# Attention over 128-token heads: output stores paired from step 8 on, and the last product cut 24 to 8

## The chip, the cores and the metric

The kernel runs on one core of a Trainium2 chip. The metric is the time of one execution on the device, in microseconds (us). The kernel before has a median of 131.08 us over five executions (130.66 to 132.13).

The core has five engines that work side by side and are held together by semaphores: TensorE (PE in the profile, with its weight loads as PEld), VectorE (DVE), ScalarE (ACT), GpSimd (POOL) and SyncE (SP), which here does nothing but issue transfers. Transfers between HBM and the on-chip memory run on 16 DMA engines. A transfer is issued by SP, ACT or POOL; in the profile the packets of SP's transfers stand under queue 1, ACT's under queue 10 and POOL's under queue 0.

## What is computed

```python
batch, n_heads, seq, head_dim = 32, 12, 128, 64      # q, k, v: float32
scale = 1.0 / np.sqrt(q.shape[-1])
scores = scale * np.matmul(q, k.transpose(0, 1, 3, 2))
scores_max = np.max(scores, axis=-1, keepdims=True)
attn = np.exp(scores - scores_max)
attn = attn / (np.sum(attn, axis=-1, keepdims=True) + 1e-8)
return np.matmul(attn, v).astype(np.float32)
```

There are 384 independent heads of 128 tokens by 64 features. Each of q, k, v and the output is 12.58 MB in float32. The kernel takes the exponential without subtracting the maximum.

## The kernel before

The 384 heads are worked off in 12 steps of 32 heads (`NDUO` = 12, so the last step is `e` = 11). In each step a tile has 128 partitions, and each partition holds 32 tokens of 64 features (`TQ` = 32). A step's output tile `o_sb` is therefore 128 x 2048 float32, 1 MB, and one store moves it (8 KB in each partition).

**Loads.** POOL issues the loads of q and k (L57) and of v (L65), which turn float32 into bf16 on the way: 512 KB arrive on the chip for every 1 MB that is read. Only the first q and k come as float32, over SP and ACT (L72). The later loads are issued by the list `later` (L99), one entry at the end of each of steps 0 to 6; the last, q11 and k11, is issued at the end of step 6.

**A step m** (the loop at L207) runs, in the order in which it is written: the first half of the scores of step m+1 (TensorE, L119, with the exponential on ACT, L124); the sums of the exponentials (TensorE L150, DVE transposes and takes the reciprocal, L172 and L174); the two halves of the output (TensorE L160, DVE transposes each into `o_sb`, L179), with the second half of the scores of step m+1 between them; pieces of the rearrangement of v for a later step (TensorE L139, ACT copies them out at L143); the transposes of q and k of step m+2 on DVE (L107); the loads of `later`; and last, POOL multiplies the whole `o_sb` by the reciprocals (L183), and some finished tiles are stored (L188).

The whole is written with a manual schedule: each engine carries out its own instructions in the order in which the program states them. An instruction that issues a store stands in the queue of the engine that issues it, and waits there for the product of the tile that it stores.

**Stores.** `held` (L192, L193) says which finished steps are stored at the end of step m, all issued by ACT:

```python
held = {m: [m - LAG] for m in range(LAG, e - 2)}      # LAG = 5, e = 11
held[e - 2], held[e - 1] = [e - 7, e - 6], [e - 5, e - 4]
```

So steps 5, 6, 7 and 8 issue the stores of tiles 0, 1, 2 and 3, step 9 those of tiles 4 and 5, and step 10 those of tiles 6 and 7. Tiles 8, 9 and 10 are stored in the last step by SP (L234, L235), which has nothing else queued: each of these is issued as soon as POOL has multiplied its tile, however early in time that is.

**The last step** cuts the product of tile 11 in two halves of 16 tokens: the first on DVE, the second on POOL (L232, L233). Each half is stored by itself, 512 KB: the first by ACT, the second by SP (L236, L237).

The tiles `o_sb` lie in a pool of `LAG + 3` = 8 buffers, shared with the two float32 loads at the start; tile m+8 reuses the buffer of tile m.

Of the kernel before, what the change touches and what calls it, by code (L numbers as in the profile page):

```python
# [10 lines left out]
def kernel(  # L11
# [12 lines left out]
    nc = tc.nc  # L24
# [6 lines left out]
    TQ = 32  # L31
# [5 lines left out]
    LAG = 5  # L37
# [31 lines left out]
    with tc.manual_schedule():  # L69
# [5 lines left out]
        def load(names):  # L75
            for name in names.split():
                kind, m = name[0], int(name[1:])
                load_v(m) if kind == "v" else load_qk(m, "qk".index(kind))
# [23 lines left out]
        def turn(m, which):  # L102


            x = chunks.pop((m, which)).bitcast(f32)
            xt = pt.tile([128, 8, S], f32, tag="qk"[which] + "t", name="qk"[which] + "t")
            nc.vector.transpose(  # L107
                xt.rearrange("p h (x g) -> p x h g", g=4),
                x if which == 0 else x.rearrange("p (y t) e -> p t y e", t=T))
            qts[m, which] = xt.bitcast(bf16).rearrange("p h (s j) -> p h s j", j=2)  # L110

        def scores(m, i):
            qt, kt = qts[m, 0], qts[m, 1]
            s_ps = ps.tile([128, 4, 4, S], f32, tag="s_ps", name="s_ps")
            for h in range(4):
                for j in range(2):
                    for b in range(4):
                        pr = slice(b * 32, (b + 1) * 32)
                        nc.tensor.matmul(  # L119
                            s_ps[:, b, h, :], lhsT=kt[pr, 4 * i + h, :, j],  # L120
                            rhs=qt[pr, 4 * i + h, :, j],
                            start=(j == 0), stop=(j == 1), tile_position=(b * 32, 0))
            attn = pa.tile([128, 4, 4, S], bf16, tag="attn", name="attn")
            nc.scalar.activation(out=attn, in_=s_ps, func=mybir.ActivationFunctionType.Exp,  # L124
                                 bias=0.0, scale=scale)
            attns[m, i] = attn

        def values(m, a, heads, half):


            v_bf = chunks[m, 2]
            ns = slice(0, 2 * CB) if half is None else slice(half * CB, (half + 1) * CB)
            if m not in v2s:
                v2s[m] = pa.tile([128, A, 2 * CB, D], bf16, tag="v2", bufs=2, name="v2")
            v_ps = ps.tile([128, heads, 4 * CB // heads, D], f32, tag="w_ps", bufs=2, name="v_ps")
            for i in range(heads):
                for tl in range(2):
                    for u in range(4):
                        nc.tensor.matmul(  # L139
                            v_ps[u * 32:(u + 1) * 32, i], lhsT=perm[:, a + i, tl, :],  # L140
                            rhs=v_bf[:, ns, 2 * u + tl, :], start=(tl == 0), stop=(tl == 1),
                            tile_position=(0, u * 32))
            nc.scalar.copy(v2s[m][:, a:a + heads, ns], v_ps)  # L143

        def denominators(m):

            d_ps = ps.tile([128, 8, S], f32, tag="w_ps", bufs=2, name="d_ps")
            for i in range(2):
                for b in range(4):
                    nc.tensor.matmul(  # L150
                        d_ps[b * 32:(b + 1) * 32, 4 * i:4 * i + 4], lhsT=ones,
                        rhs=attns[m, i][:, b], start=True, stop=True, tile_position=(0, b * 32))
            return d_ps

        def outputs(m, j):

            o_ps = ps.tile([128, 8, S], f32, tag="w_ps", bufs=2, name="o_ps")
            for h in range(8):
                for b in range(4):
                    nc.tensor.matmul(  # L160
                        o_ps[b * 32:(b + 1) * 32, h],
                        lhsT=v2s[m // 2][:, h, 4 * (m % 2) + b, j * 32:(j + 1) * 32],
                        rhs=attns[m, h // 4][:, b, h % 4],
                        start=True, stop=True, tile_position=(0, b * 32))
            return o_ps
# [4 lines left out]
        def divide(m, d_ps):  # L170
            dt = pf.tile([128, TQ, 32], f32, tag="dt", name="dt")
            nc.vector.transpose(dt, turned(d_ps))  # L172
            recip = pf.tile([128, TQ], f32, tag="recip", bufs=6, name="recip")
            nc.vector.reciprocal(recip, dt[:, :, 0])  # L174
            osbs[m] = (po.tile([128, TQ, D], f32, tag="o_sb", name="o_sb"), recip)

        def finish(m, j, o_ps):
            o_sb, _ = osbs[m]
            nc.vector.transpose(o_sb[:, :, j * 32:(j + 1) * 32], turned(o_ps))  # L179

        def scale_rows(m, eng, lo, hi):
            o_sb, recip = osbs[m]
            eng.tensor_mul(o_sb[:, lo:hi], o_sb[:, lo:hi],  # L183
                           recip[:, lo:hi].to_broadcast([128, hi - lo, D]))

        def store(m, eng, lo=0, hi=TQ):
            o_sb, _ = osbs[m]
            eng.dma_start(out=orr[:, m, lo * D:hi * D],  # L188
                          in_=o_sb[:, lo:hi].rearrange("p t d -> p (t d)"))

        e = NDUO - 1
        held = {m: [m - LAG] for m in range(LAG, e - 2)}  # L192
        held[e - 2], held[e - 1] = [e - 7, e - 6], [e - 5, e - 4]  # L193
        shuffles = {0: [(0, 0, 4, 1), (0, 4, 4, 1)],
                    1: [(1, a, 2, None) for a in range(0, A, 2)]}
        for m in range(2, NDUO // 2):
# [10 lines left out]
        for m in range(NDUO):  # L207
            todo = shuffles.get(m, [])
            if m < e:
                scores(m + 1, 0)  # L210
            divide(m, denominators(m))
            if len(todo) > 3:
                values(*todo.pop(0))
            finish(m, 0, outputs(m, 0))
            if len(todo) > 1:
                values(*todo.pop(0))
            if m < e:
                scores(m + 1, 1)
            finish(m, 1, outputs(m, 1))
            for x in todo:  # L220
                values(*x)
            if m + 2 <= e:
                turn(m + 2, 0)
                turn(m + 2, 1)
            if m < len(later):
                load(later[m])
            if m < e:
                scale_rows(m, nc.gpsimd, 0, TQ)
                for s in held.get(m, []):
                    store(s, nc.scalar)  # L230
            else:
                scale_rows(m, nc.vector, 0, TQ // 2)  # L232
                scale_rows(m, nc.gpsimd, TQ // 2, TQ)  # L233
                for s in range(e - 3, e):  # L234
                    store(s, nc.sync)  # L235
                store(m, nc.scalar, 0, TQ // 2)  # L236
                store(m, nc.sync, TQ // 2, TQ)  # L237


# [28 lines left out]
```

## Time and profile before

| What | Value |
|---|---|
| median of 5 executions | 131.08 us |
| the five | 130.66, 131.87, 132.13, 131.03, 131.08 |
| the profiled execution | 130.66 us, of which the span from first to last instruction is 128.8 us |
| busy time in the span | PE 68.5, PEld 41.5, DVE 77.7, ACT 70.7, POOL 64.4 us |
| read from HBM, written to it | 37.75 MB, 12.58 MB |
| mean granted TensorE clock | 0.885 |

Times in the trace count from the start of the span. The busy time of an engine is the time in which it carries out instructions; issuing a transfer and waiting do not count. "DMA share" is the mean busy share of the 16 DMA engines in a stretch; it can stand a little over 1 where packets overlap. "GB/s" counts the bytes at the destination, so the loads, which halve their data on the way, show about 210 GB/s where the stores show about 410.

These are the issues of all output stores, from the trace (tile, issuing engine, time of issue in us, us from issue to landing):

| Tile | By | Issued | To landing |
|---|---|---|---|
| 0 | ACT | 72.55 | 10.0 |
| 1 | ACT | 78.91 | 8.4 |
| 2 | ACT | 90.09 | 10.8 |
| 3 | ACT | 96.44 | 10.1 |
| 8 | SP | 100.53 | 7.7 |
| 4 | ACT | 107.08 | 4.0 |
| 5 | ACT | 107.46 | 8.0 |
| 9 | SP | 109.71 | 8.8 |
| 6 | ACT | 111.75 | 8.6 |
| 7 | ACT | 112.18 | 11.8 |
| 10 | SP | 117.20 | 8.1 |
| 11, first half | ACT | 121.15 | 5.4 |
| 11, second half | SP | 122.91 | 4.9 |

The last load, k11, is issued at 75.84 and lands 30.8 us later, at 106.67.

### The profile page before, as it was taken

To read this page: it belongs to the slowest core of one execution; us is meant where nothing else is said; L and a number is where in the kernel's file an instruction comes from. 1 tells how busy PE (TensorE), PEld (TensorE's weight loads), DVE (VectorE), ACT (ScalarE), POOL (GpSimd) and SP (SyncE) were. 2 spreads that over 40 slices of the span, in tenths; PEclk is the share of its full clock that TensorE was granted. 3 is DMA by queue.
4 is the path that set the end of the run, shared out by engine and by line. 5 is a ranking of instruction groups with operands and counts; after the bars stand their busy time and mean duration, and the time that the engine had idled before them with its cause. 6 is when DMAs were issued, how large, how long until landed. Compare 5 with 4: busy or idle time off the path is not lost.

```text
span 128.8 us, 4462 instructions
## 1 busy us (share of the span) xinstructions
PE 68.5 (53%) x2080; PEld 41.5 (32%) x2080; DVE 77.7 (60%) x79; ACT 70.7 (55%) x51; POOL 64.4 (50%) x52
## 2 busy tenths in 40 slices
PE   0001976657675638865189564686562886624000
PEld 0001654523333424534055251442342443413000
DVE  0128338646275968558946869557597575929600
ACT  3023795927667734977455868538673587720000
POOL 6921131316935997196692864603709209073710
PEclk9999999977999995999958999779998599995555
DMA  4999999999999999999999999999999986999990
GB/s 86 414 253 217 204 218 212 204 211 214 201 212 215 214 209 210 212 211 215 208 204 219 214 261 318 294 282 215 218 307 276 360 323 265 417 425 399 415 399 33
DMA packets 11683, 32.80 MB, mean 255 GB/s; under 512 B 784, under 2 KB 6928, under 8 KB 10000
## 3 DMA queue, kind: packets, MB, share of 16 engines
q0 software_dynamic: 9504, 17.83, 74.3%
q10 hardware_dynamic: 1440, 9.96, 19.2%
q1 hardware_dynamic: 720, 4.72, 9.5%
q8 instruction: 16, 0.26, 0.7%
q14 instruction: 3, 0.02, 0.0%
HBM read 37.75 MB, written 12.58 MB: 391 GB/s over the span
## 4 chain that ended last, share of the span: by engine, by line
DVE 35%; PE 23%; DMA 18%; ACT 7%; issue 6%; POOL 4%; POOLq 2%; ACTq 0%; DVEq 0%
DMA v_bf<-in_v_dram 18%; DVE o_sb L179 12%; PE s_ps L119 9%; DVE kt L107 8%; DVE qt L107 8%; DVE dt L172 7%; PE v_ps L139 7%; ACT attn L124 6%; PE d_ps L150 4%; PE o_ps L160 4%; POOLq L263 2%; POOL v_bf L65 1%; POOL q_bf L57 1%; POOL k_bf L57 1%; ACT v L143 1%
## 5 line engine op out<-in xcount | busy, mean ns | idle before, releaser
L124 ACT ACTIVATE attn<-s_ps 128x2048 bf16<-128x2048 f32 x24 | 45.1, 1879 | 22.8 <-PE s_ps L119 22.8
L183 POOL TENSOR_TENSOR o_sb<-o_sb,recip 128x2048 f32<-128x2048 f32 (+1 forms) x12 | 42.7, 3562 | 27.9 <-DVE o_sb L179 24.0
L119 PE MATMUL s_ps<-qt,kt 32*128 32x128 bf16 x768 | 17.1, 229 | 37.8 <-DVE kt L107 31.4
L179 DVE STREAM_TRANSPOSE o_sb<-o_ps 128x1024 f32<-128x1024 f32 x24 | 28.9, 1215 | 11.2 <-PE o_ps L160 11.2
L139 PE MATMUL v_ps<-v_bf,perm 128*32 128x512 bf16 (+1 forms) x448 | 28.9, 387 | 6.4 <-DVE dt L172 2.9
L143 ACT CAST v<-v_ps 128x1024 bf16<-128x1024 f32 x24 | 24.0, 1017 | 12.4 <-PE v_ps L139 12.4
L119 PEld LDWEIGHTS <-kt 32*128 32x128 bf16 x768 | 13.0, 98 | 46.4 <-DVE kt L107 36.1
L172 DVE STREAM_TRANSPOSE dt<-d_ps 128x1024 f32<-128x1024 f32 x12 | 15.0, 1249 | 20.7 <-PE d_ps L150 20.7
L160 PE MATMUL o_ps<-attn,v 128*32 128x128 bf16 x768 | 18.1, 239 | 3.0 <-issue 2.2
L139 PEld LDWEIGHTS <-perm 128*32 128x32 bf16 x448 | 13.4, 105 | 17.1 <-issue 12.7
L160 PEld LDWEIGHTS <-v 128*32 128x32 bf16 x768 | 14.4, 106 | 8.3 <-issue 5.5
L107 DVE STREAM_TRANSPOSE qt<-q_bf 128x1024 f32<-128x1024 f32 x12 | 14.5, 1208 | 1.2 <-DMA q_bf<-in_q_dram 1.2
L107 DVE STREAM_TRANSPOSE kt<-k_bf 128x1024 f32<-128x1024 f32 x12 | 14.5, 1206 | 1.2 <-DMA k_bf<-in_k_dram 1.2
L57 POOL DMA_DIRECT2D q_bf<-in_q_dram x11 | 6.1, 557 | 13.3 <-DMA v_bf<-in_v_dram 10.5
L57 POOL DMA_DIRECT2D k_bf<-in_k_dram x11 | 5.9, 541 | 12.4 <-DMA v_bf<-in_v_dram 7.3
L65 POOL DMA_DIRECT2D v_bf<-in_v_dram x12 | 9.4, 789 | 4.5 <-DMA k_bf<-in_k_dram 1.9
L150 PE MATMUL d_ps<-attn,ones 128*32 128x512 bf16 x96 | 9.8, 468 | 2.6 <-issue 1.5
L174 DVE RECIPROCAL recip<-dt 128x32 f32<-128x32 f32 x12 | 4.2, 353 | 0.8
L96 ACT CAST q_bf<-raw 128x1024 bf16<-128x1024 f32 x1 | 1.0, 1045 | 6.5 <-DMA raw<-in_q_dram 6.5
L95 DVE CAST q_bf<-raw 128x1024 bf16<-128x1024 f32 x1 | 0.7, 693 | 5.2 <-DMA raw<-in_q_dram 5.2
L150 PEld LDWEIGHTS <-ones 128*32 128x32 bf16 x96 | 1.7, 97 | 4.8 <-issue 3.8
L96 ACT ACT_TABLE_LOAD x1 | 1.3, 1283 | 1.2 <-PEq L252 1.2
(12 smaller groups left out, 4.6 us busy)
## 6 DMA issues: line engine op xcount, KB each, us to landing
out_dram<-o_sb ACTq DMA_DIRECT2D x8, 1024.0 KB, 9.3
v_bf<-in_v_dram POOLq DMA_DIRECT2D x12, 512.0 KB, 20.2
q_bf<-in_q_dram POOLq DMA_DIRECT2D x11, 512.0 KB, 19.7
k_bf<-in_k_dram POOLq DMA_DIRECT2D x11, 512.0 KB, 20.2
out_dram<-o_sb SPq DMA_DIRECT2D x3, 1024.0 KB, 8.1
raw<-in_k_dram ACTq DMA_DIRECT2D x1, 1024.0 KB, 8.3
raw<-in_q_dram SPq DMA_DIRECT2D x1, 1024.0 KB, 8.2
out_dram<-o_sb ACTq DMA_DIRECT2D x1, 512.0 KB, 5.4
```

What stands on the lines that cost most here:

```text
L57: nc.gpsimd.dma_start(out=x, in_=(qr, kr)[which][:, m, :].rearrange("p (t d) -> p t d", d=D))
L65: nc.gpsimd.dma_start(out=chunks[m // 2, 2][:, m % 2 * CB:(m % 2 + 1) * CB], in_=vr[:, m * CB:(m + 1) * CB, :].rearrange("p n (t d) -> p n ...
L107: nc.vector.transpose(xt.rearrange("p h (x g) -> p x h g", g=4), x if which == 0 else x.rearrange("p (y t) e -> p t y e", t=T))
L119: nc.tensor.matmul(s_ps[:, b, h, :], lhsT=kt[pr, 4 * i + h, :, j], rhs=qt[pr, 4 * i + h, :, j], start=(j == 0), stop=(j == 1), tile_positi ...
L124: nc.scalar.activation(out=attn, in_=s_ps, func=mybir.ActivationFunctionType.Exp, bias=0.0, scale=scale)
L139: nc.tensor.matmul(v_ps[u * 32:(u + 1) * 32, i], lhsT=perm[:, a + i, tl, :], rhs=v_bf[:, ns, 2 * u + tl, :], start=(tl == 0), stop=(tl == ...
L143: nc.scalar.copy(v2s[m][:, a:a + heads, ns], v_ps)
L150: nc.tensor.matmul(d_ps[b * 32:(b + 1) * 32, 4 * i:4 * i + 4], lhsT=ones, rhs=attns[m, i][:, b], start=True, stop=True, tile_position=(0, ...
L160: nc.tensor.matmul(o_ps[b * 32:(b + 1) * 32, h], lhsT=v2s[m // 2][:, h, 4 * (m % 2) + b, j * 32:(j + 1) * 32], rhs=attns[m, h // 4][:, b, ...
L172: nc.vector.transpose(dt, turned(d_ps))
L179: nc.vector.transpose(o_sb[:, :, j * 32:(j + 1) * 32], turned(o_ps))
L183: eng.tensor_mul(o_sb[:, lo:hi], o_sb[:, lo:hi], recip[:, lo:hi].to_broadcast([128, hi - lo, D]))
```

## The change

The list `held` now pairs stores from step 8 on: step 8 issues tiles 3 and 4, step 9 tiles 5 and 6, step 10 tiles 7 and 8. SP keeps tiles 9 and 10. In the last step the product is cut at 24 tokens: DVE multiplies the first 24, POOL the last 8, POOL's instruction is written first, and the two stores become 768 KB (ACT) and 256 KB (SP), SP's being written first.

```diff
         e = NDUO - 1
-        held = {m: [m - LAG] for m in range(LAG, e - 2)}
-        held[e - 2], held[e - 1] = [e - 7, e - 6], [e - 5, e - 4]
+        held = {m: [m - LAG] for m in range(LAG, e - 3)}
+        for m in range(e - 3, e):
+            held[m] = [2 * m - e - 2, 2 * m - e - 1]
...
             else:
-                scale_rows(m, nc.vector, 0, TQ // 2)
-                scale_rows(m, nc.gpsimd, TQ // 2, TQ)
-                for s in range(e - 3, e):
+                cut = 3 * TQ // 4
+                scale_rows(m, nc.gpsimd, cut, TQ)
+                scale_rows(m, nc.vector, 0, cut)
+                for s in range(e - 2, e):
                     store(s, nc.sync)
-                store(m, nc.scalar, 0, TQ // 2)
-                store(m, nc.sync, TQ // 2, TQ)
+                store(m, nc.sync, cut, TQ)
+                store(m, nc.scalar, 0, cut)
```

## The prediction

> **What bounds the kernel now.** The page says that no engine is busy for more than 60% of the span, so I read the transfers first, then the end of the span in stretches of one microsecond, and last the queue of ACT, which issues most stores. In the page's picture of the span the DMA row is the full one:
>
> ```profile
> DMA  4999999999999999999999999999999986999990
> GB/s 86 414 253 217 204 218 212 204 211 214 201 212 215 214 209 210 212 211 215 208 204 219 214 261 318 294 282 215 218 307 276 360 323 265 417 425 399 415 399 33
> ```
>
> The DMA engines are full from the second slice to the thirty-ninth (3.22 us a slice), but for one dent in slices 33 and 34. Up to the dent the loads carry it, after the dent stores alone do. The stretches around the dent and at the end (columns: stretch, length, busy time and count of PE, PEld, DVE, ACT and POOL, granted clock, DMA share and GB/s):
>
> ```profile
> 100.00:101.00 1.00, 1.00 (x20) 0.43 (x20) 0.00 (x0) 0.79 (x1) 0.51 (x1) 0.50 0.99 324
> 104.00:105.00 1.00, 1.00 (x47) 0.73 (x44) 0.32 (x1) 1.00 (x2) 0.00 (x0) 1.00 1.00 381
> 105.00:106.00 1.00, 0.67 (x19) 0.23 (x10) 1.00 (x2) 1.00 (x1) 0.00 (x0) 1.00 0.60 229
> 106.00:107.00 1.00, 1.00 (x16) 0.34 (x15) 1.00 (x2) 1.00 (x2) 0.94 (x1) 1.00 0.43 180
> 107.00:108.00 1.00, 0.03 (x4) 0.00 (x0) 1.00 (x2) 1.00 (x2) 1.00 (x1) 1.00 0.37 156
> 108.00:109.00 1.00, 0.76 (x36) 0.59 (x40) 0.18 (x1) 0.17 (x2) 1.00 (x1) 1.00 1.05 434
> 122.00:123.00 1.00, 0.00 (x0) 0.00 (x0) 0.00 (x0) 0.00 (x0) 0.88 (x1) 0.50 1.05 434
> 124.00:125.00 1.00, 0.00 (x0) 0.00 (x0) 0.00 (x0) 0.00 (x0) 0.00 (x0) 0.50 0.97 393
> 125.00:126.00 1.00, 0.00 (x0) 0.00 (x0) 0.00 (x0) 0.00 (x0) 0.00 (x0) 0.50 0.66 262
> 126.00:127.00 1.00, 0.00 (x0) 0.00 (x0) 0.00 (x0) 0.00 (x0) 0.00 (x0) 0.50 0.13 53
> ```
>
> The share falls short of 1 by 0.40, 0.57 and 0.63 in the three rows from 105 to 108: a hole of 1.60 us. From 108 to 125 it is full again; the answer for that stretch as a whole is a share of 1.01 at 410 GB/s, 6.97 MB in 17 us. That is nearly all of the 7.34 MB of the seven tiles issued from 107.08 on (4, 5, 9, 6, 7, 10 and 11). The last instruction of any engine, POOL's product, ends at 122.88, when the DMA engines still have 4.5 us of work (the last packet ends at 127.38). So the end is set by this: when the last run of stores starts (108), how many bytes it has (seven tiles, 2.5 us each), and whether it is ever starved.
>
> The share of 0.13 from 126 on is two of the sixteen DMA engines. In the packet records, most engines close their last store at 125.5 to 125.7 and two at 127.3 and 127.4; each had carried a 16 KB instruction fetch (at 113.0 and 120.2).
>
> What starts the last run is ACT's queue:
>
> ```profile
> 95.00 1.88 ACT L124 ACTIVATE attn<-s_ps 128x2048 bf16<-128x2048 f32 x1 [0.80 <-PE s_ps L119]
> 96.44 0.34 ACTq L188 DMA_DIRECT2D out_dram<-o_sb  x1
> 96.77 1.01 ACT L143 CAST v<-v_ps 128x1024 bf16<-128x1024 f32 x1
> 100.21 1.88 ACT L124 ACTIVATE attn<-s_ps 128x2048 bf16<-128x2048 f32 x1 [2.43 <-PE s_ps L119]
> ...
> 107.08 0.34 ACTq L188 DMA_DIRECT2D out_dram<-o_sb  x1
> 107.11 1.04 ACT L143 CAST v<-v_ps 128x1024 bf16<-128x1024 f32 x1
> 107.46 0.54 ACTq L188 DMA_DIRECT2D out_dram<-o_sb  x1
> ```
>
> Tile 3 is issued at 96.44; the next two stores come at 107.08, behind step 9's casts, whose matmuls run in the chain of TensorE, DVE and ACT, not behind a transfer.
>
> **The moved stores.** Tile 4 goes from 107.08 to behind tile 3, 96.8. Each later pair on ACT takes the next tiles (5 and 6 at 107.08, 7 and 8 at 111.75), and tile 8, which SP issued at 100.53, becomes the second one of step 10. Count what has been issued before the hole: before, tiles 0, 1, 2, 3 and 8; after, 0, 1, 2, 3 and 4. Five tiles both times. Issued from 107.08 on: seven tiles both times, in the same pattern (two on ACT, one on SP, two on ACT, one on SP, the last). So the loads and five stores run dry at the same moment, and the last run starts at 107.08 plus the same lead, with the same bytes. The one thing gained is that tile 4 can enter some 3.7 us before tile 8 did, but from 100 to 105 the DMA engines are at 0.99 and above: there is no idle time to fill. Worth 0.
>
> Beside it, tile 8 shared the DMA engines through a third queue while k11 was landing (106.67); now q11 and k11 have one store queue beside them, and k11 may land up to about 1 us sooner. DVE turns k11 at 106.98, straight behind its turn of q11, so it would not start sooner: 0. If k11 came later by more than 0.3 us, the scores of step 11 would move, but with 2 us to spare, as below.
>
> **ACT's queue.** One more issue in step 8, one fewer on SP. Of the eight issues of whole tiles on ACT six took 0.34 us, tile 5's 0.54 and tile 7's 1.41 (from the trace): that one found tile 5 unfinished and tile 6 just issued. Tile 4 at 96.8 will find the same: tile 2 unfinished (lands at 100.92) and tile 3 just issued. I take the 1.41, and the row that it is nearest to is that one. Behind it on ACT stands the exponential at 100.21, which waits for matmuls that end at 100.10. ACT is idle from 97.78, so the issue ends at 98.2 with 1.9 us to spare: 0. Bounds: 0.34 us (nothing) to a wait until tile 2 has landed, 100.92, which would delay the exponential by 0.8 us, and then step 9's casts and the pair at 107.08. Nothing runs sooner from it. In step 9 the same holds with 0.83 us of idle before the exponential at 108.99; tile 4 is nearly done by then, so 0.54 us is the nearest row. SP's queue loses its first store; tile 9 goes at 109.71 as before, when POOL has multiplied it.
>
> **The last product.** DVE took 1.225 us for 16 tokens, 0.077 each; POOL 3.62 us for 32, 0.113 each, so 1.81 for 16. It took 2.89, from 119.99 to 122.88: as if it had stood still while DVE multiplied (121.12 + 1.81 = 122.93). After: DVE 24 x 0.077 = 1.84, from 119.89 to 121.73; POOL 8 x 0.113 = 0.91. It ends at 122.64 if it stands still behind DVE, at 120.90 if it doesn't. I take 122.64, by the row just read. So 768 KB are issued at 121.76 (512 KB at 121.15 before), and 256 KB at 122.67 (512 KB at 122.91).
>
> Do they come late for the DMA engines? Tile 10 is closed on twelve of them at 123.0. The stores of 107.08 and 107.46 filled the queue 0.9 us after the first issue; 121.76 + 0.9 = 122.7, just in time. The remaining 256 KB have until 124.9. The two engines that end last close tile 10 at 124.8 or later, so for them there are 2 us to spare. The packets cost the same: 8 KB take 0.31 us, 4 KB 0.159, so 6 KB and 2 KB add up to one of 8 KB. Worth 0.
>
> The Trainium skill's page "DMA: Bandwidth & Descriptors", section "Anatomy of one DMA — SWDGE (gpsimd) path", fits a transfer at 2.0 us plus its bytes at 436 GB/s, for GpSimd's path. By it 768 KB would land 3.8 us after 121.76 and the kernel would end some 2 us sooner. The trace disagrees: 512 KB took 5.4 and 4.9 us where the fit gives 3.2, since they queue behind other stores. The sum goes by the trace.
>
> **The sum.** 0 + 0 + 0 against a profiled execution of 130.66 us (span 128.8, 1.9 outside it), which is the lowest of the five; against their median, 131.08, so 131.1.
>
> **The rivals.**
>
> 1. *The hole closes.* If the moved tiles filled the 1.60 us, the time would be 131.08 - 1.60 = 129.5. For it: the hole lies just where stores are moved forward. Against it: five tiles ahead of it in both kernels.
>
> 2. *ACT is held by the second store of step 8*, slower. It decides once the issue lasts past 100.10, over 3 us. Held until tile 2 lands, 0.8 us: 131.9. Held until tile 3 lands (106.54), the exponential is 6.3 us late, and so is the pair of step 9: 137.4. For it: the 1.41. Against it: that issue ended at 113.6, before tile 5 had landed at 115.4, so it needs no landing.
>
> 3. *The last piece comes late.* If POOL, now written first, multiplies first and DVE stands still behind it, DVE ends at 119.99 + 0.91 + 1.84 = 122.74, its store fills the queue at 123.6, and most engines idle 0.6 us: at most 131.7. Against it: the engines' order is not the program's; DVE started at 119.89, POOL at 119.99, behind a semaphore. The skill's page "SBUF — State Buffer", section "Who interferes with whom", has whoever issues first keep the shared port for its whole instruction; by it this rival turns on those 0.1 us.
>
> **The numbers.** What this kernel's measurement can tell from no change is about 1%, 129.77 to 132.39. No change has 0.60: 131.1, by itself 130.6 to 131.7. Rival 1 has 0.14, of which 0.01 stays within 1%. Rival 2 has 0.12, half of it at the first price, which is within 1%. Rival 3 has 0.06, all within. A loss that the rows of before don't let me see has 0.08. So faster is 0.13, within 0.60 + 0.01 + 0.06 + 0.06 = 0.73, slower 0.06 + 0.08 = 0.14. The range takes in rival 1, rival 3, and rival 2's first price with the spread of a median: 129.5 to 132.3; the dear half of rival 2, the unseen loss and the ends of the spread are left out.
>
> **What would show it.** Right: the changed profile still has a dent of some 1.6 us ahead of step 9's pair of stores, then a full DMA row to about 3 us before the end; tile 4's issue on ACT ends before 100; POOL's last product ends near 122.6, with 4 us of stores still to run. Wrong: a dent that is gone or has grown; an exponential of step 9 that waits behind an issue; a gap in the DMA row after 121.

## The result, and the profile after

The changed kernel has a median of 131.33 us (43 runs, 129.82 to 132.73), the kernel before one of 131.19 (80 runs, 130.06 to 132.86). The ratio is 0.9995, with a 95% interval of 0.9978 to 1.0012: no change. It leaves out executions over 1.5% above the fastest of their kernel, so it is not the ratio of these medians. The profiled execution of the changed kernel took 131.14 us, with a span of 129.3 us.

The page's picture of the span still has the dent in the DMA row, in the same two slices (3.23 us each):

```profile
DMA  5999999999999999999999999999999975999990
GB/s 91 412 248 216 206 221 207 204 214 211 202 216 212 217 207 208 215 215 210 205 205 218 215 248 319 282 302 216 213 326 266 373 299 246 416 421 400 416 396 32
```

By stretches (columns as before: the last two numbers are the DMA share and GB/s):

```profile
105.00:106.00 1.00, 1.00 (x24) 0.41 (x16) 0.88 (x1) 1.00 (x1) 0.00 (x0) 1.00 0.63 234
106.00:107.00 1.00, 0.58 (x14) 0.36 (x15) 1.00 (x2) 1.00 (x2) 0.49 (x1) 1.00 0.41 172
107.00:108.00 1.00, 0.47 (x12) 0.00 (x0) 1.00 (x2) 1.00 (x2) 1.00 (x1) 1.00 0.21 90
108.00:109.00 1.00, 0.32 (x24) 0.32 (x28) 0.62 (x1) 0.53 (x1) 1.00 (x1) 1.00 0.65 270
...
122.00:123.00 1.00, 0.00 (x0) 0.00 (x0) 0.03 (x1) 0.00 (x0) 0.94 (x1) 0.50 0.97 401
123.00:124.00 1.00, 0.00 (x0) 0.00 (x0) 0.00 (x0) 0.00 (x0) 0.00 (x0) 0.50 1.01 420
124.00:125.00 1.00, 0.00 (x0) 0.00 (x0) 0.00 (x0) 0.00 (x0) 0.00 (x0) 0.50 1.01 412
125.00:126.00 1.00, 0.00 (x0) 0.00 (x0) 0.00 (x0) 0.00 (x0) 0.00 (x0) 0.50 0.92 365
126.00:127.00 1.00, 0.00 (x0) 0.00 (x0) 0.00 (x0) 0.00 (x0) 0.00 (x0) 0.50 0.20 78
```

The hole is 0.37 + 0.59 + 0.79 + 0.35 = 2.10 us in this execution, 1.60 in that of before. It begins at the same time and ends half a microsecond later, since step 9's pair is issued at 107.53 and not at 107.08. Most of that shift is there before any changed instruction: tile 0 was already issued at 73.21 instead of 72.55, and ACT's second exponential of step 8 began at 95.35 instead of 95.00. From 109 on the DMA engines are full, past the last product, to about 126. The end has kept its shape too: twelve DMA engines close the last store at 126.0 to 126.1, two at 127.7 and 127.9.

On ACT, whose queue the change touches most, and at the end on DVE and POOL:

```profile
96.81 0.34 ACTq L188 DMA_DIRECT2D out_dram<-o_sb  x1
97.13 1.01 ACT L143 CAST v<-v_ps 128x1024 bf16<-128x1024 f32 x1
97.19 0.44 ACTq L188 DMA_DIRECT2D out_dram<-o_sb  x1
100.17 1.88 ACT L124 ACTIVATE attn<-s_ps 128x2048 bf16<-128x2048 f32 x1 [2.03 <-PE s_ps L119]
```

```profile
120.28 1.76 DVE L183 TENSOR_TENSOR o_sb<-o_sb,recip 128x1536 f32<-128x1536 f32 x1
```

```profile
120.37 2.56 POOL L183 TENSOR_TENSOR o_sb<-o_sb,recip 128x512 f32<-128x512 f32 x1 [2.76 <-DVE o_sb L179]
```

The second store of step 8 is issued in 0.44 us, and the exponential behind it waits for matmuls (its bracket), as before. DVE's 24 tokens took 1.76 us. POOL's eight took 2.56: DVE ends at 122.04, and POOL 0.89 us after that, at 122.93.

### The profile page after: what moved, and what is told of

Its sections match the earlier page's. It is cut to its first block, busy times and chain, and to the rows that moved or that the text cites. A ratio compares the mean times of both kernels' runs of the same rounds, so it can differ in the third digit from the quotient of the medians.

```text
span 129.3 us, 4462 instructions
## 1 busy us (share of the span) xinstructions
PE 68.0 (53%) x2080; PEld 41.1 (32%) x2080; DVE 78.2 (61%) x79; ACT 70.9 (55%) x51; POOL 64.1 (50%) x52
## 4 chain that ended last, share of the span: by engine, by line
DVE 34%; PE 23%; DMA 18%; issue 7%; POOL 6%; ACT 4%; POOLq 2%; ACTq 0%; DVEq 0%
DMA v_bf<-in_v_dram 18%; DVE o_sb L179 12%; PE s_ps L119 9%; DVE kt L107 8%; DVE qt L107 8%; PE v_ps L139 8%; DVE dt L172 6%; PE o_ps L160 4%; PE d_ps L150 3%; ACT attn L124 3%; POOL o_sb L183 3%; POOLq L265 2%; POOL v_bf L65 1%; POOL q_bf L57 1%; POOL k_bf L57 1%
## 5 line engine op out<-in xcount | busy, mean ns | idle before, releaser
L139 PE MATMUL v_ps<-v_bf,perm 128*32 128x512 bf16 (+1 forms) x448 | 30.3, 405 | 8.0 <-DVE dt L172 3.8
L160 PE MATMUL o_ps<-attn,v 128*32 128x128 bf16 x768 | 17.3, 233 | 2.7 <-issue 1.7
L160 PEld LDWEIGHTS <-v 128*32 128x32 bf16 x768 | 13.8, 103 | 7.4 <-issue 4.4
L150 PE MATMUL d_ps<-attn,ones 128*32 128x512 bf16 x96 | 8.4, 404 | 2.5 <-issue 1.4
```

The lines of the kernel that those rows point to most:

```text
L139: nc.tensor.matmul(v_ps[u * 32:(u + 1) * 32, i], lhsT=perm[:, a + i, tl, :], rhs=v_bf[:, ns, 2 * u + tl, :], start=(tl == 0), stop=(tl == ...
L150: nc.tensor.matmul(d_ps[b * 32:(b + 1) * 32, 4 * i:4 * i + 4], lhsT=ones, rhs=attns[m, i][:, b], start=True, stop=True, tile_position=(0, ...
L160: nc.tensor.matmul(o_ps[b * 32:(b + 1) * 32, h], lhsT=v2s[m // 2][:, h, 4 * (m % 2) + b, j * 32:(j + 1) * 32], rhs=attns[m, h // 4][:, b, ...
```

## The experiments

Each ratio is against the kernel before, run beside it on the same chip.

**Each part alone.** The first run has the new `held` and SP's shorter list with the old cut, the second the new cut with the old stores.

```diff
-        held = {m: [m - LAG] for m in range(LAG, e - 2)}
-        held[e - 2], held[e - 1] = [e - 7, e - 6], [e - 5, e - 4]
+        held = {m: [m - LAG] for m in range(LAG, e - 3)}
+        for m in range(e - 3, e):
+            held[m] = [2 * m - e - 2, 2 * m - e - 1]
...
-                for s in range(e - 3, e):
+                for s in range(e - 2, e):
                     store(s, nc.sync)
```

> The moved stores without the new cut of the last product (16 to 16 tokens as before). Theory (the count): five tiles are issued ahead of the hole and seven after it, as before, so no change: ratio 0.995 to 1.005, and a hole of 1.5 to 2.2 us ahead of step 9's pair. Rival (two parts that cancel): the stores gain and the new cut gives it back, so this run is 0.5% or more faster than before, and the cut alone as much slower. Rival (ACT is held): the second store's issue in step 8 takes over 1 us and the exponential of step 9 waits behind it.

Measured: 0.9999 (0.9947 to 1.0051). The hole is 1.78 us (shares of 0.63, 0.43, 0.22 and 0.94 from 105 to 109).

```diff
-                scale_rows(m, nc.vector, 0, TQ // 2)
-                scale_rows(m, nc.gpsimd, TQ // 2, TQ)
+                cut = 3 * TQ // 4
+                scale_rows(m, nc.gpsimd, cut, TQ)
+                scale_rows(m, nc.vector, 0, cut)
...
-                store(m, nc.scalar, 0, TQ // 2)
-                store(m, nc.sync, TQ // 2, TQ)
+                store(m, nc.sync, cut, TQ)
+                store(m, nc.scalar, 0, cut)
```

> The new cut (24 tokens on VectorE, 8 on GpSimd, stores of 768 and 256 KB) with the stores as before. Theory: no change, ratio 0.995 to 1.005; VectorE's product takes 1.8 us, GpSimd's ends 0.9 us after it, and the DMA engines stay full until 125. Rival (two parts that cancel): 0.5% or more slower, with a gap in the DMA row between 121 and 125. Rival (the end is the last product): GpSimd ends 0.2 to 0.3 us sooner and the time falls by that, ratio 0.998.

Measured: 1.0001 (0.9955 to 1.0048); DVE took 1.76 us, POOL 2.56. So neither part moves the time by more than about half a per cent, which leaves no room for two larger parts that cancel.

**The count of tiles ahead of the hole.** Theory: five tiles ahead of the hole in both kernels is why nothing changes. One more and one fewer must move the time.

```diff
         for m in range(e - 3, e):
             held[m] = [2 * m - e - 2, 2 * m - e - 1]
+        held[e - 1] = [e - 4]
...
-                for s in range(e - 2, e):
+                for s in range(e - 3, e):
```

> The changed kernel, but tile 8 stays with SP (issued near 100.5) and step 10 stores tile 7 alone: six tiles are issued ahead of the hole and six after it. Theory (the count): the hole of 1.6 to 2.1 us closes. k11 lands about 1.2 us later beside one more store, which the chain of step 11 has 2 us to take. Then the last product comes into play, so 1.0 to 1.6 us faster than before, ratio 0.988 to 0.992. Rival (the end is set by the last product): no gain, or a loss of up to 1.2 us from the later k11, ratio 1.000 to 1.009.

```diff
-        held = {m: [m - LAG] for m in range(LAG, e - 2)}
-        held[e - 2], held[e - 1] = [e - 7, e - 6], [e - 5, e - 4]
+        held = {5: [0], 6: [1], 7: [2], 9: [3, 4], 10: [5, 6, 7]}
```

> The kernel before, but step 8 stores nothing, step 9 tiles 3 and 4, step 10 tiles 5, 6 and 7: four tiles ahead of the hole, eight after it. Theory (the count): the DMA engines run dry one tile (2.5 us) sooner and have 2.5 us more to do after it, so the hole grows to 4.1 us and the time by 2.5 us, ratio 1.019. Rival (the end is set by the last product): the loads land sooner, the end stays, ratio 0.998 to 1.003.

Six ahead: 0.9898 (0.9756 to 1.0040), as expected in the middle, but its interval, from few executions, doesn't settle it. Its profile shows the hole gone from its old place, where the share now stays at 0.87 and above until 108, and then two smaller ones: 0.86 us from 107 to 110, and this one ahead of the last piece:

```profile
122.00:123.00 1.00, 0.00 (x0) 0.00 (x0) 1.00 (x1) 0.00 (x0) 1.00 (x1) 0.50 0.53 221
123.00:124.00 1.00, 0.00 (x0) 0.00 (x0) 0.57 (x1) 0.00 (x0) 1.00 (x1) 0.50 0.10 41
124.00:125.00 1.00, 0.00 (x0) 0.00 (x0) 0.00 (x0) 0.00 (x0) 0.47 (x1) 0.50 0.63 258
```

In that execution DVE waited 1.12 us for the load of k10, step 9's stores were issued at 108.65, and the last product ended late at 124.47.

Four ahead: 1.0262 (1.0178 to 1.0346), slower by the tile that now comes after the hole, and perhaps more. The hole has grown to 5.7 us and is empty in its middle:

```profile
103.00:104.00 1.00, 0.75 (x8) 0.32 (x11) 0.90 (x3) 0.00 (x0) 0.00 (x0) 0.50 0.63 262
104.00:105.00 1.00, 1.00 (x12) 0.18 (x4) 0.76 (x1) 0.00 (x0) 0.00 (x0) 0.50 0.41 164
105.00:106.00 1.00, 1.00 (x38) 0.78 (x35) 0.00 (x0) 0.81 (x1) 0.00 (x0) 0.56 0.06 25
106.00:107.00 1.00, 1.00 (x52) 0.78 (x48) 0.32 (x1) 1.00 (x2) 0.00 (x0) 1.00 0.00 0
```

The DMA engines run dry two microseconds sooner, as one tile less would have it; and step 9's pair was issued at 109.08 in this execution, 2.0 us later than in that of before, which is why its span is longer by 4.5 us and not by 2.5. The rival, that the last product sets the end, is excluded: it ended at 125.1 here, and the stores ran on until 131.7.

**The start of the last run, alone.** Here the five tiles ahead stay five. Only step 9's pair moves, from behind the casts to behind the exponential.

```diff
             if m < e:
                 scores(m + 1, 1)
+            if m == e - 2:
+                for s in held.pop(m):
+                    store(s, nc.scalar)
             finish(m, 1, outputs(m, 1))
```

> The changed kernel, but step 9's pair (tiles 5 and 6) is issued by ACT right behind the exponential of step 9's second scores, not behind its last casts: some 2.7 us sooner, near 104.8, when k11 has all but landed. Theory (the end is the last run of stores, from its start on): the hole closes, with the same five tiles ahead and without delaying the loads; the last run is then waiting for the last product at the end, so 0.8 to 1.6 us faster than before, ratio 0.988 to 0.994. Rival (the end is set by the last product): ratio 0.998 to 1.002, and the idle time that leaves the hole turns up in full ahead of the last piece.

Measured: 0.9822 (0.9732 to 0.9912), more than I expected, and the first of these runs to be faster than both kernels. The pair is issued at 104.32 and 104.70, and the hole is gone:

```profile
105.00:106.00 1.00, 0.78 (x16) 0.28 (x9) 1.00 (x2) 1.00 (x1) 0.00 (x0) 1.00 0.99 401
106.00:107.00 1.00, 0.90 (x16) 0.35 (x15) 1.00 (x2) 1.00 (x2) 0.81 (x1) 1.00 1.01 418
107.00:108.00 1.00, 0.15 (x4) 0.00 (x0) 1.00 (x2) 1.00 (x2) 1.00 (x1) 1.00 1.00 418
108.00:109.00 1.00, 0.64 (x36) 0.54 (x40) 0.30 (x1) 0.28 (x1) 1.00 (x1) 1.00 1.03 426
...
124.00:125.00 1.00, 0.00 (x0) 0.00 (x0) 0.00 (x0) 0.00 (x0) 0.00 (x0) 0.50 0.40 154
125.00:126.00 1.00, 0.00 (x0) 0.00 (x0) 0.00 (x0) 0.00 (x0) 0.00 (x0) 0.50 0.01 4
```

I had expected a gap ahead of the last piece in its place. There is next to none (the lowest share from 111 to 123 is 0.89): DVE began the last product at 118.35, not 119.89, though the steps up to the sums of step 11 run at the same times as before. The part on TensorE's wait, below, follows that up.

**How long an issue holds ACT** (the prediction's rival 2).

```diff
         for m in range(e - 3, e):
             held[m] = [2 * m - e - 2, 2 * m - e - 1]
+        held[e - 3], held[e - 2] = [3, 4, 5], [6]
```

> The changed kernel, but step 8 issues tiles 3, 4 and 5 on ACT and step 9 tile 6 alone: six tiles ahead of the hole. It tests how long an issue holds ACT when more than two stores are open. Theory (a third open store is what holds the issue): the first two issues take 0.34 to 0.6 us, the third over 2 us, so it ends past 100.2 and the exponential of step 9 waits behind it for 0.5 to 3 us; that eats what the closed hole brings: ratio 0.993 to 1.010. Rival (issues never hold ACT long): the third takes under 1.5 us, the exponential waits for matmuls alone, and the time is that of six tiles ahead, ratio 0.986 to 0.995. Rival 2 of the prediction in its dear form (an issue waits for a landing): the third ends only when tile 3 has landed, 105 or later, ratio above 1.03.

Measured: 0.9803 (0.9742 to 0.9865). The theory fell: the three issues took 0.34, 0.45 and 0.49 us, and the exponential of step 9 waited for matmuls. So a third open store holds nothing here, and six tiles ahead leave little of the hole (0.82 and 0.84 in the two rows from 107 to 109). The run also stores one tile, not two, in step 9; the run with one store in step 9, below, shows that this alone gains nothing.

**The slack of the last product.** GpSimd multiplies the whole of tile 11.

```diff
-                scale_rows(m, nc.gpsimd, cut, TQ)
-                scale_rows(m, nc.vector, 0, cut)
+                scale_rows(m, nc.gpsimd, 0, TQ)
...
-                store(m, nc.sync, cut, TQ)
-                store(m, nc.scalar, 0, cut)
+                store(m, nc.sync)
```

> The changed kernel, but GpSimd multiplies the whole of tile 11 (32 tokens, 3.6 us) and SP stores it as one of 1 MB. The product ends at 123.6 to 124.0, not 122.9. Theory (2 us to spare on the two DMA engines that end last, none on the others): most engines idle for about 1.2 us ahead of the last store, but it ends on them near 127 where the two late ones end anyway, so +0.1 to +0.6 us, ratio 1.000 to 1.005. Rival (the end is set by the last product): the 1.0 us by which it is later, and 0.9 to 1.5 us for the larger last store come on top, ratio 1.010 to 1.020.

Measured: 0.9991 (0.9943 to 1.0038). The product ended at 123.81 and 1 MB was issued at 123.84; the DMA engines stood idle for 1.3 us ahead of it, and no loss can be measured:

```profile
123.00:124.00 1.00, 0.00 (x0) 0.00 (x0) 0.00 (x0) 0.00 (x0) 0.81 (x1) 0.50 0.20 82
124.00:125.00 1.00, 0.00 (x0) 0.00 (x0) 0.00 (x0) 0.00 (x0) 0.00 (x0) 0.50 0.51 213
125.00:126.00 1.00, 0.00 (x0) 0.00 (x0) 0.00 (x0) 0.00 (x0) 0.00 (x0) 0.50 1.09 451
126.00:127.00 1.00, 0.00 (x0) 0.00 (x0) 0.00 (x0) 0.00 (x0) 0.00 (x0) 0.50 1.00 410
```

Its last packet ends at 127.57, that of the kernel before at 127.38. In the kernel before, twelve DMA engines close the last store by 125.7 and two at 127.3 and 127.4; here all sixteen do so between 127.2 and 127.6.

**The product by features,** on top of the moved pair: POOL takes the first 32 features while DVE transposes the others.

```diff
             finish(m, 0, outputs(m, 0))
+            if m == e:
+                scale_part(m, nc.gpsimd, 0, TQ, 0)
...
+                cut = TQ // 2
+                scale_part(m, nc.vector, 0, cut, 1)
+                scale_part(m, nc.vector, cut, TQ, 1)
...
+                store(m, nc.scalar, 0, cut)
+                store(m, nc.sync, cut, TQ)
```

> The run with step 9's pair moved forward, and the last product cut by features: GpSimd multiplies the first 32 features of all tokens while VectorE still transposes the other 32, then VectorE multiplies these in two parts of 16 tokens, and two stores of 512 KB follow at once (ACT, SP). The last piece is then issued 0.8 to 1.1 us sooner. Theory: with the hole closed the last product sets the end, so this adds 0.3 to 0.8 us to what the moved pair brings: ratio 0.983 to 0.991. Rival (the late DMA engines set the end, not the last product): no gain over the moved pair alone.

Measured: 0.9799 (0.9741 to 0.9857). That is a little below the expected 0.983 to 0.991, which its interval overlaps, and it cannot be told from the moved pair alone (0.9822, and 0.9813 when repeated), whose last packet ends at 125.15 against 125.49 here. It is no full test of the last product, though: the last piece was issued at 120.89 against 121.04, not 0.8 to 1.1 us sooner. The run gives no sign that the last product is the bound, and doesn't exclude it.

**TensorE's wait in step 11.** Where the time of the earlier last product came from shows on TensorE. The kernel before and, below it, the one with the pair moved forward, at the sums of step 11:

```profile
113.60 0.38 PE L150 MATMUL d_ps<-attn,ones 128*32 128x512 bf16 x1 [0.86 <-ACT attn L124]
115.48 0.40 PE L150 MATMUL d_ps<-attn,ones 128*32 128x512 bf16 x3 [1.51 <-issue]
```

```profile
113.71 0.62 PE L150 MATMUL d_ps<-attn,ones 128*32 128x512 bf16 x4 [0.85 <-ACT attn L124]
114.10 1.09 PE L160 MATMUL o_ps<-attn,v 128*32 128x128 bf16 x32
```

Before, TensorE stops after the first of four matmuls for 1.51 us, waiting for nothing that the profile names. In the packet records an instruction fetch of 16 KB starts at 113.02 there, and most DMA engines close the pair of step 9 at 113.0; with the pair moved, the fetch starts at 111.24 and the wait is gone. The next run keeps the hole but makes the first store behind it a single one.

```diff
         for m in range(e - 3, e):
             held[m] = [2 * m - e - 2, 2 * m - e - 1]
+        held[e - 2], held[e - 1] = [e - 6], [e - 5, e - 4, e - 3]
```

> The changed kernel, but step 9 issues tile 5 alone and step 10 tiles 6, 7 and 8, so the first store after the hole is one of 1 MB, not two. It tests the 1.5 us for which TensorE stands still in step 11's sums, near 114, where the trace shows an instruction fetch at 113.0 to 113.4, just when the pair has been drained, and the runs with no hole show the fetch at 111.2 and no such wait. Theory (the fetch stands behind the pair in the DMA engines): it starts 2 to 2.5 us sooner, near 111, TensorE's 1.5 us go, the last product starts 1.5 us sooner; the hole stays and the last run has the same bytes, so the time stays: ratio 0.995 to 1.004. Rival (the fetch's time has nothing to do with the pair): the fetch at 113 and the wait stay. Rival (the end is the last product): the time falls by 1.5 us, ratio 0.988.

Measured: 1.0036 (0.9993 to 1.0079). The fetch starts at 111.57, TensorE doesn't wait, and DVE begins the last product at 118.56 instead of 120.28:

```profile
114.14 0.40 PE L150 MATMUL d_ps<-attn,ones 128*32 128x512 bf16 x4 [0.85 <-ACT attn L124]
```

The time doesn't fall for it. So both halves of the theory hold: the pair of 2 MB holds the fetch up, and 1.7 us on the last product are worth nothing while the hole stays.

**The same edit on the kernel before,** and once more on the changed one (the edit is that of the moved pair, on each).

> The kernel before, with step 9's pair (here tiles 4 and 5) issued right behind the exponential of step 9's second scores; tile 8 stays with SP and the last product is cut 16 to 16. Theory (only the start and the length of the last run of stores count; which tiles and which cut do not): the same gain as on the changed kernel, ratio 0.977 to 0.986. Rival (the changed lists or the new cut are worth something once the hole is closed): 0.5% or more slower than the changed kernel with the pair moved, ratio 0.988 or above.

> The changed kernel with step 9's pair moved forward once more, with more rounds for a narrower interval and beside the same edit on the kernel before. Theory: ratio 0.977 to 0.986, within 0.4% of the same edit on the kernel before. Rival (the first run was favoured by chance): 0.988 or above.

Measured: 0.9815 (0.9756 to 0.9873) on the kernel before, 0.9813 (0.9762 to 0.9865) on the changed one. With the pair moved, too, the change is worth nothing that could be measured; the place of the pair is worth 1.9%. In the profiled executions of these two runs the pair went later than in the first one (105.85 and 105.35, not 104.32), and 0.7 and 0.4 us of the hole are left.

## Why the prediction was right

**The moved stores.** Worth 0, by a count of five tiles ahead of the hole in both kernels: 0.9999 alone. That the count and the start of the last run are the reason, and not luck, is shown from both sides: four ahead cost 2.6% (part of it by a later start), six ahead (the run with three stores in step 8) gained 2.0%, five with an earlier start gained 1.8 to 1.9%. The time follows the hole from one execution to the next as well. Taken as above, it is 1.60 us before (130.66 us), 1.60 with the product on GpSimd (130.79), 1.78 with the stores alone (131.03), 2.10 in the changed kernel (131.14) and 2.13 with one store in step 9 (131.34): the time less the hole is 129.0 to 129.3 us in all five, and 129.4 with four ahead.

One reading holds for the profiled execution before and not in general: that step 9's casts stand behind no transfer. With four ahead, in the first run with six ahead, and in the two repeats of the moved pair, DVE waited 1.05 to 1.17 us for k10, and step 9's stores came 0.6 to 2.0 us later than in profiles without that wait. That the one causes the other was not tried by itself.

**k11.** It was to land up to 1 us sooner, for nothing. It landed at 106.59 instead of 106.67. The term was over-sized; its worth was right.

**ACT's queue.** I took 1.41 us for tile 4's issue, from tile 7's row, because two stores were open in both places. It took 0.44, and a third open store 0.49. The number of open stores is not what made that row long; the second issue of step 10 is long again in the changed kernel (1.29 us), but what holds it stays open. The sum was not touched, since the cover was 1.9 us and the issue shorter still.

**The last product.** 1.84 and then 0.91 us were predicted, 1.76 and 0.89 measured, with POOL standing still behind DVE. It ended at 122.93, not 122.64, since DVE began 0.39 us later. The Trainium skill's page "SBUF — State Buffer", section "Who interferes with whom", states this for a VectorE instruction with two inputs in SBUF beside a GpSimd one that reads SBUF, the first to issue keeping the port; here DVE started 0.09 us ahead, though POOL's instruction stands first in the program, and POOL's extra time of 1.67 us agrees. Rival 3 did not come about.

**The spare 2 us of the two late DMA engines.** They are borne out by the run with the whole product on GpSimd: its last store was issued at 123.84, the two late engines closed tile 10 only at 124.9 and 125.1, and the 1.3 us for which the others idled cost nothing that could be measured.

**Rival 1's price was too low.** It priced the closed hole at 1.60 us, 129.5; the moved pair brought 1.9% of 131.5, 2.4 to 2.5 us. The 1.60 was the hole of one execution near the lowest of its kernel. By the 129.0 to 129.3 us above, the medians of the kernel before, 131.2 to 131.6 us in these runs, stand for a hole of 2.0 to 2.5 us (an estimate), which about covers the gain. The profiles of before and of the first run with the pair moved differ by 130.66 - 128.32 = 2.34 us, and their last packets by 127.38 - 125.15 = 2.23. The sixteen DMA engines close the last store at 125.86 in the mean before, and at 124.30 with the pair moved: 1.56 us, about the hole. The other 0.67 is that the last of them comes 1.51 us after the mean before, and 0.84 after it with the pair moved. In the two repeats of the moved pair it comes 1.33 and 1.37 us after the mean, so that share doesn't recur, and its cause stays open.

## What to carry to other kernels

When a change moves transfers, count the bytes that are issued ahead of each idle stretch of the DMA engines and behind it, and see whether the transfers that end it start any sooner: here, with both counts and that start unchanged, the time stayed, whichever tiles and queues they were. An issue in the queue of a busy engine starts where the program puts it, so the place behind the last casts was the cost here, and the same two stores ahead of them gave 1.9%. A product that ended sooner (by 1.7 us in one run) was worth nothing while stores issued earlier still filled the DMA engines.

## What was not expected of the hardware

A burst of stores holds up instruction fetches. Near step 11's sums a fetch of 16 KB started 5.9 to 6.9 us after the first issue of step 9's pair (2 MB) in every profile that has the pair: at 113.02 for 107.08 before, at 111.24 for 104.32 with the pair moved. Where step 9 stored one tile, it started 3.9 us after that issue (111.57 for 107.63). With the pair behind the casts the fetch came too late, and TensorE stood still for 1.0 to 1.8 us (1.51 before, 1.45 after, 1.77 with four tiles ahead, 1.03 with six); with one tile there, or with the pair moved forward, TensorE did not wait. That the fetch is TensorE's is concluded from this, as the packet records name no engine. The Trainium skill's page "Runtime: NRT & Kernel Launch", section "Instruction fetch mechanics", has the sequencer fetch 16 KiB blocks through its own DMA queue and calls the cost of a block boundary "mostly hidden"; these traces show a fetch whose cost was not.
